# The last eight gate tiles of a hybrid decoder trunk in four Strassen pairs, with half of the convolution's norm beside them and a second order for the head

## The chip, the cores and the metric

The kernel runs on one core of a Trainium2 chip. Times are device microseconds of one execution; the metric is their median over several runs. Differences are given to a tenth of a microsecond. PE is TensorE (matmuls), DVE is VectorE, ACT is ScalarE, POOL is GpSimd, and SP issues the DMAs.

## The reference

One layer of a decoder trunk with three gated branches, over 1024 prompt tokens, 16 meta tokens and 8x8 new tokens (after the meta tokens, 1088 columns that the later stages carry; 1104 with them):

```
u = rmsnorm(h) ;  z = u @ w_in + b_in                 # 1024 -> 6144 columns
a, c, q, k, v, g = split(z)                           # g: 3 x 1024 gate columns
y_a = pool_mixer(a)                                   # windows 2/4/8/16, group maps, scale
y_b = swish(layernorm(depthwise_conv31(glu(c)))) @ w_conv_out
y_c = sliding_window_attention(q, k, v) @ w_attn_out
h = h + (sigmoid(g0)*y_a + sigmoid(g1)*y_b + sigmoid(g2)*y_c) @ w_out
h = h + relu(rmsnorm(h) @ w_up)**2 @ w_down ;  y = rmsnorm(h)
```

All in f32: each factor is split into a high part and a low remainder (both in the fp32r type), and each product is three matmuls, hi x hi, lo x hi and hi x lo.

## The kernel before

Data lie with features on the 128 partitions and tokens along the row. The order of work is written out by hand: Python emits instructions in program order, each engine runs its own in that order, and semaphores hold an instruction until its inputs are there and the buffer that it writes is free. Buffers are `page`s of 1104 f32 out of one pool, given out in program order, so a new page waits for the last reader of the page whose place it takes.

- **Head (0 to 58 us).** `norm1(ci)` is the RMSNorm of token chunk ci (416, 320 and 368 columns) in six steps: steps 0 and 1 square the eight x tiles (L304, ACT) and add them up (L306, DVE); step 2 sums over the partitions with ones-matmuls (L260, tile `st1`), makes rstd columns on DVE, ACT and DVE (L246 to L251) and diagonal tiles of them (L266, `diag`); step 3 broadcasts them by matmuls (L271, `px`); steps 4 and 5 scale x. Between these steps stand the projections: `proj_mm(t, ci)` is the 24 matmuls of input tile t and chunk ci (L151 to L153: 8 k tiles, three matmuls each), `proj_chunk` takes the sum out of PSUM.
- **Input projection (to 706 us).** `w_in` has 48 tiles of 128 columns, each of 3 chunks of 24 matmuls. Tiles 0 to 23 are the branch inputs, 24 to 47 the gates. z tiles go to HBM (`gD`). Beside them lie the attention (`attq`: a queue of slices; `slot(n, d)` runs n slices and then d entries of `dveq`), the new tokens' attention (`sample_slices`, with `SMP` entries of `dveq` after each sequence) and the convolution's 31 taps for each of 4 tiles (`dveq`, L456 and L458: one tap). The last z tiles also split the attention's output for the next stage (`tail_slices`, tiles `oh` and `ol`), and `ln_steps` (the convolution's LayerNorm) runs after them.
- **Output maps, merge and `w_up`.** 8 tiles of `w_ao`, then `w_co`, `w_out`. `w_up` runs as 16 pairs by Strassen's identity in Winograd's form: a 2x2 block product in 7 products instead of 8, each of 24 matmuls of 272 columns (L1470 to L1473), with sums of the operands built on DVE (`sum_pair`, `prep`, L1286 to L1292, L157) and sums of the results taken on DVE (L1612 to L1618).
- **`w_down` (from 1306 us).** 7 products again, of stored operands: `op_load(n, q)` loads operand q of product n, `op_split(n, q)` splits it (`oph` on ACT, `opl` on DVE).

Of the kernel before, what the change touches and what calls it, by code (L numbers as in the profile page):

```python
# [12 lines left out]
P = 128  # L13
# [27 lines left out]
SMP = [0] * 8 + [1] * 6  # L41
# [73 lines left out]
def hybrid_trunk_kernel(ctx, tc, I, O):  # L115
# [46 lines left out]
    jobs = [(I["w_in"][i], 1024, 1 < i < NHEAD) for i in range(48)]  # L162
    WAO = [48, 49] + list(range(51, 57))
    WPOOL = 50
    jobs += [(I["w_ao"][m], 1024, False) for m in range(8)]
# [6 lines left out]
    W = Weights(nc, pool, page, jobs)  # L172
# [270 lines left out]

    def conv_steps(j):
# [17 lines left out]
    def pool_steps(g):  # L462
# [25 lines left out]
        dveq.extend([add(n, 1 << n) for n in range(g + 1)] + [fin])  # L488
# [3 lines left out]
    def ln_steps():  # L492
# [9 lines left out]
        def s2(i):  # L502
            def go():
                a, b = parts[i]
                w, acc = b - a, box["acc"][:, a:b]
                sq = [t[:, o:o + w] for t in [page("lsq") for _ in range(2)] for o in (0, 512)]
                bc = paux()[:, :b - a]
                PE.matmul(bc, lhsT=ones, rhs=acc, start=True, stop=True)
                for j in range(4):
                    V.scalar_tensor_tensor(Y[j][:, a:b], bc, -1.0 / 512, Y[j][:, a:b],  # L510
                                           ALU.mult, ALU.add)
                    A.activation(sq[j], Y[j][:, a:b], AF.Square)
                V.tensor_tensor(acc, sq[0], sq[1], ALU.add)
                V.tensor_tensor(acc, acc, sq[2], ALU.add)
                V.tensor_tensor(acc, acc, sq[3], ALU.add)
# [31 lines left out]
        return [s0, idle, idle, s2(0), s2(1), s2(2),  # L547
                idle, idle, s4(0), s4(1), s4(2), s5(0), s5(1), s5(2)], [s6(j) for j in range(4)]
# [99 lines left out]
    def att_slices(qd):  # L648
# [21 lines left out]
        for n in range(8 * qd, 8 * qd + 8):  # L670
# [3 lines left out]
            out += [(even(n, not first), 1), (odd(n, not first), 1)]  # L674
# [5 lines left out]
    def sample_slices():  # L680
# [3 lines left out]
        def build():  # L684
# [43 lines left out]
        def qk(sq):  # L728
# [7 lines left out]
            lg = page("slg")[:, :192]  # L736
# [119 lines left out]
    def proj_open(ti):  # L856
# [74 lines left out]
    def proj_close(ti):  # L931
# [31 lines left out]
        elif kind == "q":  # L963
# [79 lines left out]
    def tail_slices():  # L1043
        both = lambda *fs: (lambda: [f() for f in fs])
        idle = lambda: None
        pairs = [load_split(Ox, "o", oD[j]) for j in range(8)]
        out = [both(pairs[j][0], pairs[j + 1][0]) for j in (0, 2)]
        for j in range(0, 8, 2):
            fs = [pairs[j][1], pairs[j + 1][1]]
            fs += [pairs[j + 4][0], pairs[j + 5][0]] if j + 4 < 8 else []  # L1050
            out.append((both(*fs), 1))
        return out
# [117 lines left out]
    for m in range(8):  # L1170
# [95 lines left out]


    raws, Ssum, WX = {}, {}, {}
    ORD = ("A11", "S1", "S2", "S4", "S3", "A12", "A22")

    def load_pair(j):
        raws[j] = []
        for f in (2 * j, 2 * j + 1):
            t = page2("wra")[:, :1024] if j % 2 == 0 else \
                pool.tile([P, 1024], F32, name="wraw", tag="wraw", bufs=2)
            SP.dma_start(t, I["w_up"][f])
            raws[j].append(t)

    def sum_pair(j, n):
        a, b = raws[j]  # L1280
        if n == 0:
            Ssum[j] = page2("s12"), page2("s34")
        s12, s34 = Ssum[j]
        S1, S2, S3, S4 = s12[:, :512], s12[:, 512:1024], s34[:, :512], s34[:, 512:1024]
        if n == 0:
            V.tensor_tensor(S1, b[:, :512], b[:, 512:], ALU.add)  # L1286
        elif n == 1:
            V.tensor_tensor(S2, S1, a[:, :512], ALU.subtract)
        elif n == 2:
            V.tensor_tensor(S4, a[:, 512:], S2, ALU.subtract)  # L1290
        else:
            V.tensor_tensor(S3, a[:, :512], b[:, :512], ALU.subtract)  # L1292

    def prep(s):
        j, i = divmod(s, 7)
        a, b = raws[j]
        s12, s34 = Ssum[j]
        src = {"A11": a[:, :512], "A12": a[:, 512:], "A22": b[:, 512:], "S1": s12[:, :512],
               "S2": s12[:, 512:1024], "S3": s34[:, :512], "S4": s34[:, 512:1024]}[ORD[i]]
        tag = ("whi", "wlo")[s % 2]  # L1300
        t = pool.tile([P, 1024], F32R, name=tag, tag=tag, bufs=2)
# [674 lines left out]
```

## Time and profile before

| | |
|---|---|
| median of 3 runs | 1661.78 us (1661.28 to 1661.79) |
| profiled execution | 1662.0 us |
| its span, first to last instruction | 1660.1 us |
| granted TensorE clock, mean | 0.995 |
| busy PE / DVE / ACT | 1642.7 / 1134.5 / 750.5 us |

PE is busy for 99% of the span; the other two engines have room on average, but not everywhere. The profiled execution is 1.9 us longer than its span and 0.2 us longer than the median. Idle time of PE, and matmuls that cost more than their columns, are the two places in which a change shows.

### The profile page before, as it was taken

To read this page: it belongs to the slowest core of one execution; us is meant where nothing else is said; L and a number is where in the kernel's file an instruction comes from. 1 tells how busy PE (TensorE), PEld (TensorE's weight loads), DVE (VectorE), ACT (ScalarE), POOL (GpSimd) and SP (SyncE) were. 2 spreads that over 40 slices of the span, in tenths; PEclk is the share of its full clock that TensorE was granted. 3 is DMA by queue.
4 is the path that set the end of the run, shared out by engine and by line. 5 is a ranking of instruction groups with operands and counts; after the bars stand their busy time and mean duration, and the time that the engine had idled before them with its cause. 6 is when DMAs were issued, how large, how long until landed. Compare 5 with 4: busy or idle time off the path is not lost.

```text
span 1660.1 us, 28943 instructions
## 1 busy us (share of the span) xinstructions
PE 1642.7 (99%) x11568; PEld 1618.2 (97%) x11568; DVE 1134.5 (68%) x2120; ACT 750.5 (45%) x1428; POOL 5.8 (0%) x14
## 2 busy tenths in 40 slices
PE   9999999999999999999999999999999999999997
PEld 8999999999999999999999999999999999999997
DVE  7786767867776666455584687777777844457674
ACT  6537667467675342364243343233332533333341
POOL 0000000000000000000000000000000000000000
PEclk9999999999999999999999999999999999999998
DMA  6051221231225353344253447777776955556652
GB/s 207 15 110 52 71 79 42 68 77 41 81 63 173 97 197 113 104 184 146 80 172 124 152 162 242 244 237 246 243 241 227 323 194 184 183 184 222 204 173 85
DMA packets 132123, 250.78 MB, mean 151 GB/s; under 512 B 33459, under 2 KB 64148, under 8 KB 131988
## 3 DMA queue, kind: packets, MB, share of 16 engines
q1 hardware_dynamic: 131428, 248.45, 46.2%
q8 instruction: 91, 1.49, 0.4%
q10 hardware_dynamic: 560, 0.48, 0.1%
q14 instruction: 44, 0.36, 0.1%
HBM read 168.52 MB, written 80.36 MB: 150 GB/s over the span
## 4 chain that ended last, share of the span: by engine, by line
PE 95%; DVE 2%; ACT 1%; DMA 1%; issue 0%; SPq 0%; DVEq 0%; ACTq 0%
PE pm L151 13%; PE pm L153 13%; PE pm L152 13%; PE m L1663 7%; PE m L1665 7%; PE m L1667 7%; PE m L1470 6%; PE m L1473 6%; PE m L1472 6%; PE pn L151 3%; PE pn L153 3%; PE pn L152 3%; PE px L634 2%; PE px L622 2%; PE qk L581 2%; PE px L271 1%
## 5 line engine op out<-in xcount | busy, mean ns | idle before, releaser
L151 PE MATMUL pm<-uh,whi 128*128 128x320 f32 (+3 forms) x1008 | 338.5, 336 | 0.6 <-ACT uh L342 0.5
L153 PE MATMUL pm<-uh,wlo 128*128 128x320 f32 (+3 forms) x1008 | 333.1, 330 | 0.0
L152 PE MATMUL pm<-ul,whi 128*128 128x320 f32 (+3 forms) x1008 | 332.2, 330 | 0.6 <-DVE ul L343 0.6
L1663 PE MATMUL m<-oph,whi 128*128 128x272 f32 (+2 forms) x896 | 258.5, 289 | 0.0
L1665 PE MATMUL m<-opl,whi 128*128 128x272 f32 (+2 forms) x896 | 258.0, 288 | 0.0
L1667 PE MATMUL m<-oph,wlo 128*128 128x272 f32 (+2 forms) x896 | 257.8, 288 | 0.0
L93 ACT ACTIVATE whi<-wraw 128x1024 fp32r<-128x1024 f32 (+1 forms) x127 | 130.0, 1025 | 205.6 <-PE m L1665 138.3
L94 DVE TENSOR_TENSOR wlo<-wraw,whi 128x1024 fp32r<-128x1024 f32 (+1 forms) x127 | 150.6, 1187 | 98.3 <-ACT whi L93 98.3
L151 PEld LDWEIGHTS pm<-uh,whi 128*128 128x128 f32 x1008 | 190.8, 189 | 2.6 <-ACT uh L342 1.3
L152 PEld LDWEIGHTS pm<-ul,whi 128*128 128x128 f32 x1008 | 191.3, 190 | 1.9 <-DVE ul L343 1.5
L153 PEld LDWEIGHTS pm<-uh,wlo 128*128 128x128 f32 x1008 | 190.3, 189 | 0.4
L1665 PEld LDWEIGHTS m<-opl,whi 128*128 128x128 f32 x896 | 168.8, 188 | 0.0
L1663 PEld LDWEIGHTS m<-oph,whi 128*128 128x128 f32 x896 | 168.6, 188 | 0.0
L1667 PEld LDWEIGHTS m<-oph,wlo 128*128 128x128 f32 x896 | 168.5, 188 | 0.0
L456 DVE SCALAR_TENSOR_TENSOR y<-ext,vec,y 128x1024 f32<-128x1024 f32 x120 | 152.5, 1271 | 0.0
L1470 PE MATMUL m<-bch,wlo 128*128 128x272 f32 x448 | 129.2, 288 | 2.0 <-DVE cb L1614 2.0
L1470 PE MATMUL m<-bch,whi 128*128 128x272 f32 x448 | 129.3, 289 | 0.6 <-DVE h L1409 0.6
L1473 PE MATMUL m<-bch,whi 128*128 128x272 f32 x448 | 128.9, 288 | 0.0
L1473 PE MATMUL m<-bch,wlo 128*128 128x272 f32 x448 | 128.8, 288 | 0.0
L1472 PE MATMUL m<-bcl,whi 128*128 128x272 f32 x448 | 128.7, 287 | 0.0
L1472 PE MATMUL m<-bcl,wlo 128*128 128x272 f32 x448 | 128.7, 287 | 0.0
L1470 PEld LDWEIGHTS m<-bch,wlo 128*128 128x128 f32 x448 | 84.2, 188 | 2.2 <-issue 2.2
(364 smaller groups left out, 3418.1 us busy)
## 6 DMA issues: line engine op xcount, KB each, us to landing
wraw<-w_in SPq DMA_DIRECT2D x46, 512.0 KB, 3.9
opT<-d SPq DMA_DIRECT2D x64, 272.0 KB, 3.0
ld<-opT SPq DMA_DIRECT2D x32, 544.0 KB, 4.6
wd<-w_down SPq DMA_DIRECT2D x32, 512.0 KB, 5.8
sumD<-wd SPq DMA_DIRECT2D x32, 512.0 KB, 4.3
wraw<-sumD SPq DMA_DIRECT2D x32, 512.0 KB, 3.6
gt<-gD SPq DMA_DIRECT2D x24, 544.0 KB, 4.7
ld<-opB SPq DMA_DIRECT2D x23, 544.0 KB, 4.7
```

The costliest lines, as they stand in the source:

```text
L93: self.nc.scalar.activation(hi, r, AF.Copy)
L94: self.late.append(lambda lo=lo, r=r, hi=hi: self.nc.vector.tensor_tensor(lo, r, hi.bitcast(F32), ALU.subtract))
L151: PE.matmul(ps, lhsT=wh[k], rhs=xh, start=first and i == 0, stop=False)
L152: PE.matmul(ps, lhsT=wh[k], rhs=xl, start=False, stop=False)
L153: PE.matmul(ps, lhsT=wl[k], rhs=xh, start=False, stop=last and i == n - 1)
L456: V.scalar_tensor_tensor(y[:, :NP], e[:, k:k + NP], w, y[:, :NP], ALU.mult, ALU.add)
L1470: PE.matmul(ps, lhsT=wh, rhs=xh, start=first and k == 0, stop=False, skip_group_check=True)
L1472: PE.matmul(ps, lhsT=wh, rhs=xl, start=False, stop=False, skip_group_check=True)
L1473: PE.matmul(ps, lhsT=wl, rhs=xh, start=False, stop=k == 3, skip_group_check=True)
L1663: PE.matmul(ps, lhsT=wh[:, w], rhs=xh[:, r], start=k == 0, stop=False, skip_group_check=True)
L1665: PE.matmul(ps, lhsT=wh[:, w], rhs=xl[:, r], start=False, stop=False, skip_group_check=True)
L1667: PE.matmul(ps, lhsT=wl[:, w], rhs=xh[:, r], start=False, stop=k == 15, skip_group_check=True)
```

## The change

1. The z tiles 40 to 47 (gate tiles) become 4 pairs by the same Strassen form as `w_up`: for each pair 7 products of 24 matmuls of 272 columns. Their operands are sums of halves of u over tokens (`z_sums`: 16 DVE operations over four k), split into hi and lo parts (`z_split`; T1 is written over the upper token half of the pages Uh and Ul of k 0 to 3), and sums of weight blocks (`sum_pair`, `prep`). Results go out of PSUM by ACT copies and DVE adds (L1318, L1320, L1322).
2. The attention's odd slots run 2 entries of `dveq` instead of 1; the sample section's `SMP` goes from [0]*8 + [1]*6 to [1]*8 + [2]*6.
3. The loads and splits of the attention's output go from the z tiles into the last pair and the first `w_ao` tile, which for that runs by k over three PSUM banks.
4. `ln_steps` is cut in halves. Its sums and squares (`s0`, six `s2`) run beside the pairs, the rest during `w_ao`.
5. Small tiles move into pages; the attention's pool is closed, and `pool2` opened, before the pairs.
6. In the head, `proj_chunk(3, 0)` and `proj_mm(0, 1)` go ahead of `n1[2]`, `n2[0]`, `n2[1]`, and `proj_mm(2, 1)` ahead of `n1[3]`, `n2[2]`.
7. `op_split(0, 4)` to `(0, 6)` and `op_load(1, 1)` go from the last `w_up` pair into the start of `w_down`.

```diff
-SMP = [0] * 8 + [1] * 6
+SMP = [1] * 8 + [2] * 6
+
+NZP = 4
+NZ = 48 - 2 * NZP
...
-            out += [(even(n, not first), 1), (odd(n, not first), 1)]
+            out += [(even(n, not first), 1), (odd(n, not first), 2)]
...
+    def z_sums(k):
+        ua, ub = zt[k] = page("zu"), page("zu")
+        lo, hi = slice(0, HL), slice(HL, L)
+        for t, n in ((ua, k), (ub, k + 4)):
+            V.tensor_tensor(t[:, :L], Uh[n][:, NM:].bitcast(F32), Ul[n][:, NM:].bitcast(F32),
+                            ALU.add)
+        V.tensor_tensor(ua[:, lo], ua[:, hi], ua[:, lo], ALU.subtract)
+        V.tensor_tensor(ua[:, hi], ub[:, hi], ua[:, hi], ALU.subtract)
+        V.tensor_tensor(ub[:, hi], ub[:, hi], ua[:, lo], ALU.subtract)
+        V.tensor_tensor(ub[:, lo], ub[:, lo], ub[:, hi], ALU.subtract)
...
+        if x == "T1":
+            split(Uh[k][:, NM + HL:], Ul[k][:, NM + HL:], ua[:, lo])
...
+    proj_chunk(3, 0, b0_[3])
+    b1_ = [proj_mm(0, 1)]
     n1[2]()
     n2[0]()
     n2[1]()
-    proj_chunk(3, 0, b0_[3])
-    b1_ = [proj_mm(0, 1)]
     proj_chunk(4, 0, b0_[4])
     b1_.append(proj_mm(1, 1))
+    b1_.append(proj_mm(2, 1))
     n1[3]()
     n2[2]()
-    b1_.append(proj_mm(2, 1))
...
+    load_pair(1 - NZP)
+    for k in range(4):
+        z_split("T1", k)
+    prep(-7 * NZP + 2)
...
+    for s in range(-7 * NZP, 0):
+        j, i = divmod(s, 7)
...
+        if s + 3 < 0:
+            prep(s + 3)
+        if j < -1 and 2 <= i < 6:
+            sum_pair(j + 1, i - 2)
+        b = bk[(0, 1, 0, 1, 0, 2, 0)[i]]
+        product(b, s, i, i in (0, 1, 5), z_comb)
...
+            if i < 3:
+                A.activation(d, ps, AF.Copy)
+            elif i == 6:
+                A.activation(d, ps, AF.Identity, bias=bias_col[1])
+            else:
+                V.scalar_tensor_tensor(d, ps, bias_col[i == 4], d, ALU.add, ALU.add)
...
+            for n in ((), (), (0, 1), (2,), (3,), (4,), (5,))[i]:
+                oq[n][1]()
+            for n in ((0, 1, 2), (), (3, 4), (5,), (6,), (7,), ())[i]:
+                oq[n][0]()
...
+        slot(1, 2)
...
+                if n == q == 0:
+                    op_split(0, 4)
+                    op_load(1, 1)
+                    op_split(0, 5)
+                    op_split(0, 6)
```

**In the head, PE.** Before, the broadcast of chunk 1's rstd (`px_557`, from `diag_482`), the sums over chunk 2's squares (`st1_562`), 24 matmuls of `proj_mm(2, 1)` (`pn_580`), and the broadcast of chunk 2's rstd (`px_611`):

```order
L153 MATMUL pm_532<-uh7_116,wlo_218 128x320
L271 MATMUL px_557<-diag_482,ones_93 128x128 x3
L260 MATMUL st1_562<-ones_93,sq_437 128x1 x3
L151 MATMUL pn_580<-uh0_109,whi_251 128x320
L152 MATMUL pn_580<-ul0_117,whi_251 128x320
...
L153 MATMUL pn_580<-uh7_116,wlo_252 128x320
L271 MATMUL px_611<-diag_576,ones_93 128x128 x3
L151 MATMUL pn_639<-uh0_109,whi_300 128x320
```

After, the same place, where `pn_557` is `proj_mm(2, 1)` and `px_582` is chunk 1's broadcast:

```order
L155 MATMUL pn_557<-ul7_124,whi_251 128x320
L156 MATMUL pn_557<-uh7_116,wlo_252 128x320
L273 MATMUL px_582<-diag_510,ones_93 128x128 x3
L262 MATMUL st1_587<-ones_93,sq_437 128x1 x3
L273 MATMUL px_611<-diag_601,ones_93 128x128 x3
L154 MATMUL pn_639<-uh0_109,whi_300 128x320
```

The 24 matmuls have moved from between `st1` and the second `px` to ahead of the first `px`, so that the three small groups stand next to each other.

**In the head, ACT.** The squares of chunk 2's eight tiles with the engines that each waits for, before:

```order
L304 ACTIVATE sq_437<-x_404 128x368 [waits DMAHW0_49,Activation_49]
L304 ACTIVATE sq_437<-x_404 128x368 x2
L304 ACTIVATE sq_438<-x_406 128x368 [waits DMAHW1_49,Activation_49]
L304 ACTIVATE sq_438<-x_406 128x368 x2
L304 ACTIVATE sq_439<-x_408 128x368 [waits DMAHW2_49,PE_49]
```

and after:

```order
L306 ACTIVATE sq_437<-x_404 128x368 [waits DMAHW0_49,PE_49]
L306 ACTIVATE sq_437<-x_404 128x368 x2
L306 ACTIVATE sq_438<-x_406 128x368 [waits DMAHW1_49,PE_49,Activation_49]
L306 ACTIVATE sq_438<-x_406 128x368 x2
L306 ACTIVATE sq_439<-x_408 128x368 [waits DMAHW2_49,DVE_49]
```

The three pages `sq_437`, `sq_438` and `sq_439` have come to other places in the pool: `sq_438` (squares 4 to 6) and `sq_439` (squares 7 and 8) now take the place of `diag_510`, which PE's `px_582` reads, and `sq_439` also waits for DVE's adds of the squares before it.

**At the entry into the pairs, DVE.** Before, the row between two z tiles holds taps and one weight split. After, this stands there, from the last z tile to the second product; `za` belongs to product 2, `ul` with `zu` is T1, `whi` and `wlo` of 128x512 are the weight operands of products 1 to 4:

```order
L160 TENSOR_TENSOR za_6977<-zu_6802,za_6976 128x544 [waits Activation_49]
L160 TENSOR_TENSOR za_6981<-zu_6867,za_6980 128x544 [waits Activation_49]
L160 TENSOR_TENSOR wlo_6984<-s12_6907,wlo_6984 128x512 [waits PE_49,Activation_49]
L160 TENSOR_TENSOR ul0_117<-zu_6609,uh0_109 128x544 [waits PE_49,Activation_49]
L160 TENSOR_TENSOR ul1_118<-zu_6717,uh1_110 128x544 [waits PE_49,Activation_49]
L160 TENSOR_TENSOR ul2_119<-zu_6801,uh2_111 128x544 [waits PE_49,Activation_49]
L160 TENSOR_TENSOR ul3_120<-zu_6866,uh3_112 128x544 [waits PE_49,Activation_49]
L160 TENSOR_TENSOR whi_7004<-s12_6907,whi_7004 128x512 [waits PE_49,Activation_49]
L1096 TENSOR_TENSOR s34_7007<-wraw_6875,s12_6907 128x512
L1098 TENSOR_TENSOR s34_7007<-wraw_6875,wraw_6877 128x512
L160 TENSOR_TENSOR wlo_7014<-s34_7007,wlo_7014 128x512 [waits PE_49,Activation_49]
```

All of these are new there; each row that waits for "Activation" has an ACT split of the same tile ahead of it, and the T1 rows wait for PE to have read the last z tile's u.

**In pair 2, DVE.** This stands there after (nothing of it before; the norm's steps L526 to L532 then ran during `w_ao`): L526 subtracts the mean, L532 adds squares that ACT made of it, `wlo` and `whi` are weight splits behind ACT, L1094 and L1096 are weight sums, L1322 empties a product's banks:

```order
L526 SCALAR_TENSOR_TENSOR y_3669<-px_7337,y_3669 128x384
L526 SCALAR_TENSOR_TENSOR y_4632<-px_7337,y_4632 128x384
L160 TENSOR_TENSOR wlo_7380<-wra_6994,wlo_7380 128x512 [waits PE_49,Activation_49]
L1094 TENSOR_TENSOR s12_7346<-s12_7346,wraw_7186 128x512 [waits DMAHW1_49,DVE_49]
L1322 SCALAR_TENSOR_TENSOR zc_7264<-zp_7303,b_in_91,zc_7264 128x272 [waits PE_49]
L1322 SCALAR_TENSOR_TENSOR zc_7264<-zp_7304,b_in_91,zc_7264 128x272 [waits PE_49]
L532 TENSOR_TENSOR lacc_7190<-lacc_7190,lsq_7374 128x384 [waits DVE_49] x2
L526 SCALAR_TENSOR_TENSOR y_272<-px_7413,y_272 128x320 [waits PE_49]
L526 SCALAR_TENSOR_TENSOR y_1857<-px_7413,y_1857 128x320
L160 TENSOR_TENSOR whi_7419<-wraw_7186,whi_7419 128x512 [waits Activation_49]
L1096 TENSOR_TENSOR s34_7422<-wraw_7186,s12_7346 128x512
L1322 SCALAR_TENSOR_TENSOR zc_7265<-zp_7266,b_in_91,zc_7265 128x272 [waits PE_49]
```

The evictions of a product have come to stand behind a weight split that waits for ACT, which has two squares to make first.

## Rows read from the trace of the kernel before

**Rows 1.** The page's first parts: the span, busy time and instructions of each engine, and the chain that ended last by engine.

```profile
span 1660.1 us, 28943 instructions
PE 1642.7 (99%) x11568; PEld 1618.2 (97%) x11568; DVE 1134.5 (68%) x2120; ACT 750.5 (45%) x1428; POOL 5.8 (0%) x14
...
PE 95%; DVE 2%; ACT 1%; DMA 1%; issue 0%; SPq 0%; DVEq 0%; ACTq 0%
```

**Rows 2.** PE's waits: tile and line that waited, the engine, tile and line waited for, us in total, times, longest.

```profile
PE m L1470 <- DVE cb L1614: 2.0, 1, 2.0
...
PE st L260 <- DVE sq L306: 1.1, 1, 1.1
PE pn L151 <- DVE gt L1165: 0.8, 1, 0.8
```

**Rows 3.** PE in order of time: the first matmul of a z tile and of the next one; below them the first matmul of a 272-column product of `w_up` and of the next.

```profile
609.99 0.34 PE L151 MATMUL pm<-uh,whi 128*128 128x400 f32 x1
...
621.90 0.34 PE L151 MATMUL pm<-uh,whi 128*128 128x400 f32 x1
...
1021.63 0.28 PE L1470 MATMUL m<-bch,whi 128*128 128x272 f32 x1
...
1024.65 0.29 PE L1470 MATMUL m<-bch,wlo 128*128 128x272 f32 x1
```

**Rows 4.** The head, PE's small groups in order of time.

```profile
34.68 0.80 PE L260 MATMUL st<-ones,sq 128*128 128x1 f32 x6 [1.13 <-DVE sq L306]
44.03 0.83 PE L271 MATMUL px<-diag,ones 128*128 128x128 f32 x6
44.70 0.73 PE L260 MATMUL st<-ones,sq 128*128 128x1 f32 x6
48.90 0.83 PE L271 MATMUL px<-diag,ones 128*128 128x128 f32 x6
```

**Rows 5.** The head, ACT's squares of chunk 2, and DVE's adds of them, evictions and rstd chain, each in order of time.

```profile
37.01 3.30 ACT L304 ACTIVATE sq<-x 128x368 f32<-128x368 f32 x8
...
38.53 4.41 DVE L306 TENSOR_TENSOR sq<-sq 128x368 f32<-128x368 f32 x7
...
45.47 0.16 DVE L246 TENSOR_SCALAR st<-st 128x3 f32<-128x3 f32 x1 [1.54 <-PE st L260]
...
46.70 0.68 DVE L266 TENSOR_SCALAR diag<-ident,st 128x128 f32<-128x128 f32 x3
```

**Rows 6.** Windows: busy us of PE, PEld, DVE, ACT and POOL (with instructions), granted clock, DMA share, GB/s.

```profile
32.00:36.00 4.00, 2.87 (x19) 2.57 (x18) 3.37 (x8) 1.53 (x4) 0.00 (x0) 0.97 0.00 0
36.00:40.00 4.00, 4.00 (x19) 4.00 (x18) 2.92 (x12) 3.88 (x11) 0.00 (x0) 0.60 0.01 2
40.00:44.00 4.00, 4.00 (x29) 4.00 (x28) 3.51 (x7) 0.78 (x2) 0.00 (x0) 1.00 0.00 0
...
1300.00:1304.00 4.00, 1.98 (x16) 1.79 (x16) 4.00 (x6) 1.62 (x2) 0.00 (x0) 1.00 1.03 415
```

**Rows 7.** Attention, DVE in order of time: a tap (L456 and L458) with what follows it.

```profile
147.19 0.43 DVE L587 CUSTOM_DVE_ANT_0 lg<-qk,bias 128x256 f32<-128x256 f32 x1 [1.57 <-PE qk L581]
...
156.95 1.25 DVE L456 SCALAR_TENSOR_TENSOR y<-ext,vec,y 128x1024 f32<-128x1024 f32 x1
158.12 0.28 DVE L458 SCALAR_TENSOR_TENSOR y<-exts,vec,y 128x64 f32<-128x64 f32 x1
158.32 1.22 DVE L94 TENSOR_TENSOR wlo<-wraw,whi 128x1024 fp32r<-128x1024 f32 x1
159.45 0.41 DVE L587 CUSTOM_DVE_ANT_0 lg<-qk,bias 128x256 f32<-128x256 f32 x1
```

**Rows 8.** The sample section in windows, columns as in rows 6.

```profile
500.00:520.00 20.00, 20.00 (x127) 20.00 (x126) 17.95 (x35) 9.50 (x26) 0.00 (x0) 1.00 0.60 186
520.00:540.00 20.00, 20.00 (x134) 20.00 (x133) 10.61 (x51) 10.01 (x31) 0.00 (x0) 1.00 0.57 168
540.00:560.00 20.00, 20.00 (x131) 19.93 (x130) 11.14 (x47) 10.20 (x30) 0.00 (x0) 1.00 0.44 135
560.00:580.00 20.00, 20.00 (x128) 18.73 (x128) 14.76 (x21) 3.78 (x7) 0.00 (x0) 1.00 0.20 65
```

**Rows 9.** Groups of one shape on ACT and DVE, with busy us, mean ns of one and idle time before them: splits of 544 and 512, copies, squares, and the norm's operations.

```profile
L156 ACT ACTIVATE bch<-u 128x544 fp32r<-128x544 f32 x12 | 7.4, 645 | 0.0
L156 ACT ACTIVATE whi<-wraw 128x512 fp32r<-128x512 f32 x8 | 5.0, 623 | 0.0
L928 ACT ACTIVATE zs<-pn,b_in 128x400 f32<-128x400 f32 x4 | 2.4, 596 | 9.6 <-issue 8.8 <-ACT whi L93 0.8
L512 ACT ACTIVATE lsq<-y 128x384 f32<-128x384 f32 x8 | 3.8, 524 | 1.3 <-DVE y L510 1.3
L157 DVE TENSOR_TENSOR wlo<-s,wlo 128x512 fp32r<-128x512 f32 x32 | 22.0, 686 | 0.0
L500 DVE TENSOR_TENSOR lacc<-lacc,y 128x1088 f32<-128x1088 f32 x2 | 2.6, 1294 | 0.1
L510 DVE SCALAR_TENSOR_TENSOR y<-px,y 128x384 f32<-128x384 f32 x8 | 3.9, 550 | 6.7 <-PE px L508 6.7
```

**Rows 10.** The end of `w_up` and the start of `w_down`: PE's first matmul of `w_down`; ACT's loads waited for; DVE in order of time.

```profile
1306.06 0.29 PE L1663 MATMUL m<-oph,whi 128*128 128x272 f32 x1
...
1299.39 1.12 ACT L156 ACTIVATE oph<-ld 128x1088 fp32r<-128x1088 f32 x1 [2.96 <-DMA ld<-opB]
...
1313.34 0.73 DVE L1510 TENSOR_TENSOR d<-cb,d 128x544 f32<-128x544 f32 x1
1313.98 0.72 DVE L1511 TENSOR_TENSOR d<-cb,ca 128x544 f32<-128x544 f32 x1
1314.62 0.72 DVE L1517 TENSOR_TENSOR d<-cb,d 128x544 f32<-128x544 f32 x1
```

More of the change, by code (lines that the diff above doesn't have):

```diff
@@ L160, in hybrid_trunk_kernel @@
     ctx.enter_context(sched)
[L162 to L165, printed above, removed]
+    W = Weights(nc, pool, page, [(I["w_in"][i], 1024, 1 < i < NHEAD) for i in range(NZ)])
+    WAO = [0, 1] + list(range(3, 9))
+    WPOOL = 2
+    jobs = [(I["w_ao"][m], 1024, False) for m in range(8)]
     jobs.insert(WPOOL, (I["w_pool"], 1024, True))
@@ L442, in hybrid_trunk_kernel, with small @@
     sig, ext, Y, ea = {}, {}, {}, {}
+    smalls = {}
+    def small(j, off, n):
+        if j not in smalls:
+            smalls[j] = page("xs")
+        return smalls[j][:, off:off + 8 * n].rearrange("p (s t) -> p s t", s=8)
     def conv_steps(j):
@@ L470, in go @@
                 if n < 2:
-                    box[n] = (page("pt"), apool.tile([P, 8, 23], F32, name="pts", tag="pts", bufs=2))
+                    box[n] = (page("pt"), small(g, 488 + 184 * n, 23))
                 cur, curs = box[(n - 1) % 2] if n else (e, es)
@@ L487, in fin @@
             store(rD[g], r[:, :L])
-        dveq.extend([add(n, 1 << n) for n in range(g + 1)] + [fin])
+        fs = [add(n, 1 << n) for n in range(g + 1)] + [fin]
+        if g == 3:
+            dveq[:0] = fs
+        else:
+            dveq.extend(fs)
     Sx = []
@@ L1041, in load_split, with page2 @@
         return ld, sp
[L1043 to L1052, printed above, removed]
+    def page2(name):
+        return pool2.tile([P, T], F32, name=name, tag="page2", bufs=5)
@@ new lines, in product @@
+    def product(b, s, i, first, op):
+        t = WX.pop(s)
+        for ch in range(2):
+            for k in range(4):
+                wh, wl = (t[:, o + 128 * k:o + 128 * k + 128] for o in (0, 512))
+                xh, xl = op(BX[i], k, ch)
+                ps = b[ch][:, :HL // 2]
+                PE.matmul(ps, lhsT=wh, rhs=xh, start=first and k == 0, stop=False,
+                          skip_group_check=True)
+                PE.matmul(ps, lhsT=wh, rhs=xl, start=False, stop=False, skip_group_check=True)
+                PE.matmul(ps, lhsT=wl, rhs=xh, start=False, stop=k == 3,
+                          skip_group_check=True)
@@ L1146, in hybrid_trunk_kernel @@
             slot(1, NDVE[0] if attq else NDVE[1])
         proj_close(ti)
-    while len(Ox) < 8:
+    while attq:
         slot(1, 1)
+    slot(0)
+    apool_ctx.__exit__(None, None, None)
+    pool2 = ctx.enter_context(tc.tile_pool(name="sb2", bufs=1, reuse_waits="tile"))
+    load_pair(1 - NZP)
+    for k in range(4):
+        z_split("T1", k)
+    prep(-7 * NZP + 2)
+    for n in (2, 3):
+        sum_pair(-NZP, n)
+    for x in ("T3", "T4"):
+        attq.extend(lambda x=x, k=k: [z_split(x, k), z_split(x, k + 1)] for k in (0, 2))
@@ L1265, in comb @@
         return tuple(t[:, o:o + HL // 2] for t in BC[x, k // 2])
[L1268 to L1301, printed above, removed]
-        split(t[:, :512], t[:, 512:], src)
-        WX[s] = t
-        if i == 6:
-            raws.pop(j)
-            Ssum.pop(j)
     sqa = page("sqa")
```

241 lines of the change are left out of this document (178 added, 63 removed).

## The prediction

> **What bounds the kernel now.** I read the page's busy times first: PE works for 1642.7 of 1660.1 us, and PE is 95% of the chain that ended last [rows 1]. So time leaves only through fewer or shorter matmuls, and comes only where PE waits or runs at a lower clock. The view of PE's waits comes next: the longest single one is 2.0 us, and the few above 0.5 us are named there [rows 2]. That is the state in which most of DVE's and ACT's work is hidden, and the question for this change is whether it stays hidden when about 100 DVE and ACT instructions are put beside fewer matmuls. Last I read, stretch by stretch, the head, the attention, the sample section and the two ends of `w_up` in time order.
>
> **The gain.** In the z tiles the first matmul of one tile starts at 609.99 and that of the next at 621.90 [rows 3]: 11.9 us for 72 matmuls. A product of 24 matmuls of 272 columns goes from 1021.63 to 1024.65, 3.0 us [rows 3]. Two tiles are 23.8 us, a pair's seven products 21.1 us. Four pairs: 4 x (23.8 - 21.1) = 10.8; with an even 125 ns for a matmul a pair is 21.0 and the sum 11.3. The starts are rounded to 0.01 us, which is 0.3 over 28 products; I take 11, and 10.5 and 11.7 as bounds. **-11.0.**
>
> The Trainium skill gives another price: "TensorE: Matmul & The Clock Gate", section "Wait — 56ns, not 53.3ns?", has start-to-start of warm matmuls at N / 2.4 GHz + about 2.5 ns. By it a tile would be 11.1 us and a pair 19.5, a gain of 10.6 (an estimate from that page). The trace's 3.02 us for 24 is longer than that rule's 2.78, so here the trace decides, and the sum differs by 0.4.
>
> **The head.** This is in the changed order alone and I am surest of it. Before, PE runs `px` at 44.03, `st` at 44.70, 24 matmuls to 48.90, then the second `px` [rows 4]; nothing waits there.
> - *First stall.* After, `sq_438` and `sq_439` take the place of `diag_510`, so squares 4 to 8 wait for `px_582`. That now stands behind `proj_mm(2, 1)`, directly ahead of `st1_587`, which needs all eight squares added up. What was done in 37.01 to 42.94 beside matmuls [rows 5] now begins when `px_582` ends. Eight squares take 3.30 us, 0.40 each; seven adds take 4.41, 0.63 each [rows 5]. From `px_582`: a square 0.5, adds 4 to 6 in 3 x 0.57 to 0.63, then squares 7 and 8 wait for these adds (0.5), then two adds 1.1 to 1.2: 3.8 to 4.0. **+3.9**, from 0 (were the buffers freed otherwise) to 4.4.
> - *Second stall.* `px_611` follows `st1_587` with no matmuls between. The rstd chain goes from `st`'s end at 45.43 (44.70 + 0.73) to the last `diag` at 46.70 + 0.68 = 47.38 [rows 4, 5]: 1.95 us, covered before by the 24 matmuls, which go up to 48.90. **+2.0**, from 1.5 to 2.6. Those 24 matmuls are not saved: they stand earlier.
> - *Clock.* PE waited 1.13 us before `st` at 34.68; then 36 to 40 us had a granted clock of 0.60 [rows 4, 6]. That stretch did 2.4 us of full-rate work in 4. The 1.13 us wait stays in the changed order, as the matmuls now there wait for the same DVE evictions. A drop after the two new stalls is another (1 - 0.60) x 4 = **+1.6**, from 0 to 3.2: the 2.0 us wait in 1300 to 1304 left a clock of 1.00 [rows 6], so a wait need not bring one.
>
> **Attention.** An odd slot runs a second tap. A tap with its L458 takes 1.4 us by starts (156.95 to 158.32 [rows 7]). Between two visits of the unit's chain to DVE it has room where DVE was idle: 1.57 us ahead of `lg` at 147.19 covers a whole tap [rows 7]. After the tap at 156.95 a weight split and `lg` follow with no gap [rows 7]; there the next `lg`, and the transposes on PE behind it, come 1.4 us later. I count two such places that PE feels: **+2.8**, from 0 to 6. What is put earlier here is taken from a stretch in which PE does not wait, so it gives nothing back.
>
> **Sample section.** 14 more taps, 14 x 1.4 = 19.6 us of DVE, into 500 to 580 us, where DVE is busy for 17.95, 10.61, 11.14 and 14.76 of each 20 [rows 8], 54.5 of 80. In the mean they fit (25.5 free), but DVE is visited several times by each sequence's chain, so a tap delays a visit where it stands ahead of one. Two taps' worth again: **+2.8**, from 0 to 5.
>
> **Entry into the pairs.** T1 overwrites pages that the last z tile reads, so its splits can't start before that tile ends. On ACT then stand the tile's eviction (0.6), two `za` splits (0.57 each), a weight split (0.53) and four T1 splits (0.57 each), these being the durations of [rows 9] less the 0.09 by which neighbours overlap, then DVE's last remainder (0.72): 5.3 us, with the semaphores between some 5.9. Product 0 hides 3.0, and product 1 reads T1's fourth k after 10 matmuls more, 1.25: a wait of about 1.6. Product 2 goes to product 0's banks, whose ACT copies stand behind all that: 0.6 more, and small ones of 0.3. **+2.5**, from 0.5 to 5.
>
> **Pairs 1 to 3.** In pair 1 DVE has 14 splits of 544 (0.64 each, the pitch of [rows 10]), 12 operations of 512 (0.60), four evictions of 272 (0.41, an estimate: 550 ns for 384 and 0.72 us for 544 [rows 9, 10] drawn down to 272) and the norm's three adds of 1088 (1.21): 8.9 + 7.2 + 1.6 + 3.6 = 21.4 us in 21.0 of PE, begun 1.4 late. The three adds stand right ahead of the ones-matmul that sums them, which waits in PE's queue with all products behind it: 1.0. In pair 2 each product has a loop: two mean subtractions (0.47), two squares on ACT behind the first (0.5 each), then ACT's weight split 0.57, DVE's remainder 0.6, a weight sum 0.6, two evictions 0.8, two adds 0.9: about 5 us against 3.0 of PE [rows 3, 9]. Product 6 needs banks that L1322 empties at the end of this loop: 3.0. **+4.0**, from 0 (if the weight splits run ahead) to 8.
>
> **Elsewhere.** `w_ao` has a 0.8 us wait already [rows 2]; the by-k order adds **+0.3**. In `w_down`, `op_split(0, 4)` comes behind the sums of the last pair: 1314.62 + 0.7 [rows 10], less the three splits of 1.2 that no longer stand ahead of them, 1311.7; its own 1.28 gives 1312.9 to 1313.1. PE has 48 matmuls from 1306.06 [rows 10], 6.0 us, and wants it at 1312.1, or a little earlier as the 2.0 wait ahead stays [rows 2]. **+1.0**, from 0 to 2. Costed at nothing: the moved sizes and pages (item 5), which add no instructions, and `z_sums` in the z tiles: 16 operations, 4 x (2 x 1.21 + 4 x 0.64) = 20 us of DVE, over four tiles of 11.9 us, where the taps that are now done earlier (1.4 each) stood; without that cover it would be up to 8.
>
> **The sum.** -11.0 + 3.9 + 2.0 + 1.6 + 2.8 + 2.8 + 2.5 + 4.0 + 0.3 + 1.0 = +9.9. I take +9.5, the stalls being partly the same time (a late DVE in pair 1 is late already from the entry). Span 1669.6, with the 1.9 outside it 1671.5 for a profiled execution; the median is 0.2 lower: **1671 us**.
>
> **The rivals.** A measurement tells 0.2% (3.3 us): faster means under 1658.5, slower over 1665.1.
> - *As forecast* (1666 to 1676): chance 0.50.
> - *The pairs hide their work* (the other side). ACT and DVE have room on average (45% and 68% [rows 1]); if the weight splits run three products ahead of PE, the loop of pair 2 has three products, 9 us, to be late in, and taps lie in idle time. Then only the head and the entry are left: -11.0 + 3.9 + 2.0 + 1.6 + 2.5 = -1.0, 1660.8: not slower. It decides at 3.0 us of loop per product, less whatever lead the splits have. The banks speak against it: they are emptied by rows behind those splits, whatever the lead. Chance 0.13, and 0.03 for a head that is hidden too (1653).
> - *The clock falls again at later stalls.* The windows show one drop after a wait of 1.13 us and none after 2.0 [rows 6]. With stalls at the entry, in pairs 1 and 2 and at `w_down`, four drops at 1.6 add 6.4: 1677.5. Chance 0.22. The Trainium skill, "TensorE: Matmul & The Clock Gate", section "HAM oscillation — how this bites in real kernels", has idle gaps return the gate to half rate; the 0.60 after the head's wait agrees, the 1.00 around 1303 does not.
> - *The late loads.* The last pair's loads of the attention's output compete with four weight loads and stores. ACT waited 2.96 us for such a load at 1299.39 [rows 10]; here its product copies stand behind the split that waits, so one or two such waits reach PE through the banks: +3 to +6, 1675.5. Chance 0.12.
>
> **The numbers.** The range goes from 1662 to 1681: below it stay the two cases in which the work is hidden (0.15), above it only a sum of the second and third rivals. Forecast alone: 1666 to 1676. Faster 0.06, same 0.11, slower 0.83: the case of hidden pairs (1660.8) lies within 0.2%, a quarter of it below, with the hidden head.
>
> **What would show it.** In the profile after: PE waits at `st` L262 for DVE `sq` (about 3.9) and at `px` L273 for `diag` (about 2.0) around 50 us, and a granted clock under 0.7 in the 4 us behind; a wait of L1126 for `ul` or `za` right after the last z tile; waits of the pairs' products for L1322 or L1318; 21.0 us between pairs where they run free. If PE's waits outside the head add up to under 3 us the second rival is right and I am wrong by some 10 us; if the pairs' products take more than 3.0 us where nothing is waited for, the gain is too large in my sum.

## The result, and the profile after

The changed kernel takes 1676.93 us (median of 4, 1675.98 to 1677.95) against 1661.78: slower, ratio 1.0091 with a 95% interval of 1.0073 to 1.0108, so 15 us with 12 to 18. That lies in the range (1662 to 1681), but above the forecast's own 1666 to 1676, and next to the rival in which the clock falls again (1677.5).

The page after (first parts and the chain), which answers to [rows 1]:

```profile
span 1674.2 us, 29251 instructions
PE 1642.2 (98%) x11664; PEld 1612.7 (96%) x11664; DVE 1191.9 (71%) x2220; ACT 767.5 (46%) x1475; POOL 5.7 (0%) x14
...
PE 86%; DVE 7%; ACT 3%; issue 2%; DMA 1%; SPq 0%; DVEq 0%; ACTq 0%
```

PE has 96 matmuls more and as much busy time, and the span is 14.1 us longer: what was added is waiting, and busy time at a lower clock. DVE and ACT have gone from 3% to 10% of the chain that ended last. PE's waits after, which answer to [rows 2]:

```profile
PE st L262 <- DVE sq L308: 4.3, 1, 4.3
PE m L1814 <- DVE opl L160: 3.4, 1, 3.4
PE px L273 <- DVE diag L268: 3.4, 2, 1.7
PE m L1124 <- DVE cb L1765: 2.6, 1, 2.6
PE zp L1124 <- DVE zc L1322: 2.2, 1, 2.2
PE pm L154 <- DVE un L927: 1.6, 1, 1.6
...
PE str L781 <- DVE os L776: 1.0, 1, 1.0
PE px L524 <- DVE lacc L513: 0.9, 1, 0.9
PE zp L1126 <- DVE ul L160: 0.6, 1, 0.6
```

Each wait that the prediction named as a sign is there. When PE comes to the same point of the program in the two traces shows where the time went:

| PE starts | before | after | behind by |
|---|---|---|---|
| the bias matmul after the head | 81.25 | 88.71 | 7.5 |
| the first matmul of the sample section | 516.26 | 526.27 | 10.0 |
| z tile 40, or the first product | 609.99 | 623.25 | 13.3 |
| `w_ao` | 711.07 | 716.25 | 5.2 |
| `w_up` | 963.26 | 971.88 | 8.6 |
| `w_down` | 1306.06 | 1315.53 | 9.5 |
| the end of the span | 1660.1 | 1674.2 | 14.1 |

From `w_ao` to `w_up` the 3.4 us are mostly no loss: the norm's six small groups of matmuls ran among the z tiles before and run here now.

The head after, PE in order of time, which answers to [rows 4]:

```profile
35.01 0.42 PE L154 MATMUL pm<-uh,whi 128*128 128x320 f32 x1 [1.58 <-DVE un L927]
38.66 0.72 PE L262 MATMUL st<-ones,sq 128*128 128x1 f32 x6
46.41 0.83 PE L273 MATMUL px<-diag,ones 128*128 128x128 f32 x6
51.52 1.25 PE L262 MATMUL st<-ones,sq 128*128 128x1 f32 x6 [4.28 <-DVE sq L308]
54.47 1.62 PE L273 MATMUL px<-diag,ones 128*128 128x128 f32 x6 [1.70 <-DVE diag L268]
```

The three groups stand side by side, and before the second and the third of them PE is idle. ACT's squares of chunk 2 in the same stretch:

```profile
47.32 1.31 ACT L306 ACTIVATE sq<-x 128x368 f32<-128x368 f32 x3 [6.30 <-issue]
49.73 0.91 ACT L306 ACTIVATE sq<-x 128x368 f32<-128x368 f32 x2 [1.10 <-DVE sq L308]
```

Squares 4 to 6 begin 0.08 us after the first broadcast ends (46.41 + 0.83), after 6.30 us of idle time, and squares 7 and 8 wait for DVE's adds, in the order that the reused pages ask for (the view names no releaser for the first of the two: "issue"). Windows after, columns as in [rows 6], for the head, the end of the sample section, pair 2 and the start of `w_down`:

```profile
48.00:52.00 4.00, 0.48 (x4) 0.49 (x4) 3.06 (x6) 1.54 (x4) 0.00 (x0) 0.97 0.01 2
52.00:56.00 4.00, 2.30 (x11) 2.24 (x12) 2.30 (x10) 2.01 (x5) 0.00 (x0) 0.50 0.00 0
56.00:60.00 4.00, 4.00 (x21) 4.00 (x21) 3.67 (x8) 2.21 (x5) 0.00 (x0) 0.68 0.06 13
...
576.00:580.00 4.00, 4.00 (x21) 4.00 (x21) 4.00 (x6) 0.00 (x0) 0.00 (x0) 0.67 0.04 12
...
670.00:674.00 4.00, 4.00 (x22) 4.00 (x23) 2.94 (x8) 2.40 (x5) 0.00 (x0) 0.63 0.01 4
...
1322.00:1326.00 4.00, 0.77 (x3) 0.77 (x4) 4.00 (x5) 2.31 (x3) 0.00 (x0) 0.86 0.00 0
1326.00:1330.00 4.00, 4.00 (x26) 4.00 (x25) 4.00 (x5) 1.12 (x1) 0.00 (x0) 0.71 0.86 235
```

The clock is under 1.00 not only behind the head's waits but at three later places; with the neighbouring windows each comes to some 1.7 us of full-rate work not done, 4 x (0.14 + 0.29) for the last one. Two of them begin with the end of a wait, that of 2.2 us in pair 2 and that of 3.4 us in `w_down`. The one at the end of the sample section does not: the wait of 1.0 us is long over there, and what stands directly ahead is a group of 15 small matmuls (`spv`, 574.34 to 576.68).

```profile
565.55 0.33 PE L781 MATMUL str<-ident,os 128*128 128x128 f32 x1 [1.02 <-DVE os L776]
...
574.34 0.49 PE L793 MATMUL spv<-spt,VSh 64*128 64x512 f32 x1
...
577.45 0.51 PE L155 MATMUL pm<-ul,whi 128*128 128x368 f32 x1
```

From 577.4 us on a matmul of 368 columns takes 0.51 us; just before it was 0.33.

### The profile page after: what moved, and what is told of

Same layout as the page of the kernel before. It is cut to its first block, busy times and chain, and to the rows that moved or that the text cites. A ratio compares the mean times of both kernels' runs of the same rounds, so it can differ in the third digit from the quotient of the medians.

```text
span 1674.2 us, 29251 instructions
## 1 busy us (share of the span) xinstructions
PE 1642.2 (98%) x11664; PEld 1612.7 (96%) x11664; DVE 1191.9 (71%) x2220; ACT 767.5 (46%) x1475; POOL 5.7 (0%) x14
## 4 chain that ended last, share of the span: by engine, by line
PE 86%; DVE 7%; ACT 3%; issue 2%; DMA 1%; SPq 0%; DVEq 0%; ACTq 0%
PE pm L154 10%; PE pm L156 10%; PE pm L155 10%; PE m L1814 7%; PE m L1812 7%; PE m L1816 7%; PE m L1124 6%; PE m L1127 6%; PE m L1126 6%; PE pn L154 2%; PE pn L155 2%; PE pn L156 2%; PE px L653 2%; PE px L641 2%; PE qk L600 2%
## 5 line engine op out<-in xcount | busy, mean ns | idle before, releaser
L154 PE MATMUL pm<-uh,whi 128*128 128x320 f32 (+3 forms) x912 | 306.3, 336 | 1.9 <-DVE un L927 1.6
L156 PE MATMUL pm<-uh,wlo 128*128 128x320 f32 (+3 forms) x912 | 301.7, 331 | 0.0
L155 PE MATMUL pm<-ul,whi 128*128 128x320 f32 (+3 forms) x912 | 301.5, 331 | 0.1
L96 ACT ACTIVATE whi<-wraw 128x1024 fp32r<-128x1024 f32 (+1 forms) x119 | 121.7, 1024 | 193.1 <-PE m L1814 142.3
L97 DVE TENSOR_TENSOR wlo<-wraw,whi 128x1024 fp32r<-128x1024 f32 (+1 forms) x119 | 140.8, 1184 | 81.8 <-ACT whi L96 81.8
L154 PEld LDWEIGHTS pm<-uh,whi 128*128 128x128 f32 x912 | 172.8, 189 | 4.1 <-DVE un L927 1.9
L155 PEld LDWEIGHTS pm<-ul,whi 128*128 128x128 f32 x912 | 172.9, 190 | 1.9 <-DVE ul L345 1.6
L156 PEld LDWEIGHTS pm<-uh,wlo 128*128 128x128 f32 x912 | 172.5, 189 | 0.4
```

What stands on the lines that cost most here:

```text
L96: self.nc.scalar.activation(hi, r, AF.Copy)
L97: self.late.append(lambda lo=lo, r=r, hi=hi: self.nc.vector.tensor_tensor(lo, r, hi.bitcast(F32), ALU.subtract))
L154: PE.matmul(ps, lhsT=wh[k], rhs=xh, start=first and i == 0, stop=False)
L155: PE.matmul(ps, lhsT=wh[k], rhs=xl, start=False, stop=False)
L156: PE.matmul(ps, lhsT=wl[k], rhs=xh, start=False, stop=last and i == n - 1)
```

## The experiments

All are held against the kernel before in the same session, by ratio; differences to the changed kernel are of medians.

**The changed kernel once more.** No edit.

> The changed kernel itself, unedited, with more runs beside the kernel before, as the measure that the single edits are held against. From the profile's ledger: PE's waits and the late half-rate stretches cost it 14 us of span against before, so a ratio of 1.0085 to 1.009 (1676 to 1677.5 us). If the half-rate stretches behind its waits at 577, 670 and 1325 us come and go between executions, as the edited kernels let suppose, its runs spread over some 3 to 5 us and the waits stay the same to 0.1 us with other stretches behind them.

Measured: 1677.96 us (1675.88 to 1679.76), ratio 1.0094, 1.0077 to 1.0111. The waits are those above to 0.1 us, but for `opl` with 3.7 and one at the very start (`uh`, 0.9 instead of 0.3), and the clock differs. Two windows of this run:

```profile
576.00:580.00 4.00, 4.00 (x26) 4.00 (x26) 4.00 (x6) 0.00 (x0) 0.00 (x0) 1.00 0.00 0
...
670.00:674.00 4.00, 4.00 (x25) 4.00 (x25) 3.72 (x8) 2.12 (x5) 0.00 (x0) 0.70 0.21 85
```

After the same small matmuls at the end of the sample section the clock stays at 1.00 here and was 0.67 above. The waits belong to the program; where a lower clock follows is in part a matter of the execution.

**The head's order undone.**

```diff
-    proj_chunk(3, 0, b0_[3])
-    b1_ = [proj_mm(0, 1)]
     n1[2]()
     n2[0]()
     n2[1]()
+    proj_chunk(3, 0, b0_[3])
+    b1_ = [proj_mm(0, 1)]
     proj_chunk(4, 0, b0_[4])
     b1_.append(proj_mm(1, 1))
-    b1_.append(proj_mm(2, 1))
     n1[3]()
     n2[2]()
+    b1_.append(proj_mm(2, 1))
```

> The changed kernel with the head in the order of before, all else as changed. Theory of the sum: the head's two stalls (4.3 and 1.7 us in the changed kernel's profile) and one of its two half-rate stretches go, 7.0 to 7.5 us less than the changed kernel, about 1669.5 us; PE's stalls for sq and diag around 50 us are gone. Rival, the pages alone: the moved buffers (item 5) keep the squares behind the broadcast whatever the order; then only the 1.7 us stall goes, about 1674.

Measured: 1667.19 us, ratio 1.0029 (1.0019 to 1.0039), 10 under the changed kernel. The two stalls are gone; of `sq` a wait of 0.21 is left. The order accounts for the loss in the head, and the rival falls. The 2 to 3 us more than expected fit the clock of the profiled execution: this trace has no window under 1.00 in the head (before had one of 0.60), and its wait in pair 2 stands with a full clock behind it. Against that, the wait at the start of `w_down` has grown from 3.4 to 4.4 us.

```profile
658.65 0.36 PE L1124 MATMUL zp<-zb,wlo 128*128 128x272 f32 x1 [2.18 <-DVE zc L1322]
...
660.00:664.00 4.00, 3.82 (x31) 3.61 (x30) 2.91 (x7) 3.06 (x8) 0.00 (x0) 1.00 0.00 0
```

**The head's order alone,** on the kernel before: the same lines the other way round.

> The kernel before with the new order of the head alone. If both stalls come from the order: 7 us over before, about 1669. If the first stall needs the moved pages of item 5 as well, and the second comes from the order: PE waits some 2 us for diag and not for sq, 1.7 to 3.5 us over before (the upper end with a half-rate stretch behind it), 1663.5 to 1665.3.

Measured: 1664.8 us, ratio 1.0019 (1.0010 to 1.0028), about 3 over before. PE waits 1.70 us for `diag` at 51.24 and nowhere for `sq`; the clock stays at 1.00 in 48 to 56. So the second stall is the order's own, and the first needs both the order and the other parts' pages. Which of the small tiles moved into pages decides it was not tried.

**The head's second move undone,** in the changed kernel.

```diff
     b1_.append(proj_mm(1, 1))
-    b1_.append(proj_mm(2, 1))
     n1[3]()
     n2[2]()
+    b1_.append(proj_mm(2, 1))
```

> The changed kernel with proj_mm(2, 1) alone back between the sums of chunk 2 and the second broadcast. Theory of two separate stalls: the 4.3 us wait for sq stays (the squares still need the page that the first broadcast reads), the 1.7 us wait for diag goes: 1.7 less than the changed kernel and up to 1.7 more if the half-rate stretch is shorter, 1673.5 to 1675.2. Rival, one stall: with the matmuls back both go, 6 us less, about 1671.

Measured: 1675.46 us, ratio 1.0070 (1.0055 to 1.0084), 1.5 to 2.5 under the changed kernel. That is just above the expected times, and the six executions spread over 5.5 us (1671.47 to 1676.94), so the waits decide it and not the time. The wait for `sq` is still 4.3, that for `diag` in the head is gone (1.7 of 3.4 is left: that of the final norm, which the kernel before has too). Two separate stalls, as the theory has it.

**The taps alone,** on the kernel before.

```diff
-SMP = [0] * 8 + [1] * 6
+SMP = [1] * 8 + [2] * 6
...
-            out += [(even(n, not first), 1), (odd(n, not first), 1)]
+            out += [(even(n, not first), 1), (odd(n, not first), 2)]
```

> The kernel before with the two numbers that set the taps alone (second tap in the odd slots, the longer list in the sample section). Theory: by PE's milestones the changed kernel lost 2.6 us in the attention and 1.5 in the sample section besides a half-rate stretch; the same shows here, 4.1 over before, to 5.8 with the stretch: 1666 to 1668. Rival, the taps only hurt with the changed pages: within 1.5 us of before.

Measured: 1667.64 us, ratio 1.0027 (1.0018 to 1.0036), 4.5 us over before: the taps' places cost what the table of starting times says (2.5 us in the attention, 3.3 in the sample section, of which 1.7 is the lower clock there), without any of the rest of the change. PE's waits of over 0.1 us between 140 and 600 us in this run:

```profile
PE str L757 <- DVE slg L752: 1.1, 1, 1.1
PE px L622 <- ACT lg L613: 0.3, 1, 0.3
PE px L634 <- DVE pl L157: 0.2, 1, 0.2
```

They add up to less than half of it. The rest lies mostly in the attention, between the small matmuls of the `px` groups: from one to the next of them, 463 times, PE takes 2.0 us more in all than in the kernel before, and few of these gaps are long enough to be listed as waits. The profiled execution, at 1668.11 us, also has a lower clock around 995 us, far from the taps.

**The operand splits back in the last `w_up` pair.**

```diff
-            if i < 4:
+            if i < 5:
                 op_split(0, i)
-            if i < 5:
                 op_load(0, i + 2)
             elif i == 5:
+                op_split(0, 5)
+                op_split(0, 6)
                 op_load(1, 0)
+                op_load(1, 1)
...
-                if n == q == 0:
-                    op_split(0, 4)
-                    op_load(1, 1)
-                    op_split(0, 5)
-                    op_split(0, 6)
```

> The changed kernel with the three operand splits and the load back in the last w_up pair. Theory: the 3.4 us wait at the start of w_down and the 1.7 us that the half-rate stretch behind it costs go, and 0.6 of the wait ahead of it: 5.1 to 5.7 less, about 1671.5. Rival, the late weight tile: the landing that ACT waits 9.4 us for holds the chain either way, and the wait only moves to another operand: within 1.5 us of the changed kernel.

Measured: 1671.64 us, ratio 1.0053 (1.0041 to 1.0066), 5.3 to 6.3 under the changed kernel: the size that the theory gives, and the rival falls. The wait for `opl` is gone. What is left at this place is 2.8 us, on ACT's `oph` in the last pair; the 0.6 us ahead of it did not go, as this wait was 2.6 in the changed kernel. In the profiled execution the lower clock did not go either (0.50 in 1312 to 1316 us, 0.65 in the 4 us behind); it was the slowest of the five, at 1673.89.

**`w_down`'s second weight tile split later.**

```diff
             elif i == 4:
                 W.load_to(3)
-            elif i == 5:
-                W.split_to(2)
-                W.flush()
```

> The changed kernel with the split of w_down's second weight tile after the last pair instead of ahead of its square. Theory of the late tile: in the changed kernel DVE waits 2.7 us for that split (ACT 9.4 us for the landing) ahead of the chain to operand 4; without it there the wait of PE at the start of w_down falls from 3.4 to about 1.0: 2.4 less, 4 with the half-rate stretch gone. Rival, the three operand splits themselves (4.9 us of DVE behind the sums) make the wait: it stays above 3.

Measured: 1673.44 us, ratio 1.0061 (1.0049 to 1.0073), some 4 under the changed kernel; the wait is 2.1, neither 1.0 nor over 3. DVE and ACT around it, in order of time:

```profile
1315.68 1.29 DVE L1627 SCALAR_TENSOR_TENSOR ca<-ca 128x1088 f32<-128x1088 f32 x1
1320.56 0.73 DVE L160 TENSOR_TENSOR opl<-ca,oph 128x544 fp32r<-128x544 f32 x1 [3.59 <-ACT oph L159]
...
1325.08 1.22 DVE L97 TENSOR_TENSOR wlo<-wraw,whi 128x1024 fp32r<-128x1024 f32 x1
...
1319.36 0.62 ACT L1771 ACTIVATE cb<-m 128x544 f32<-128x544 f32 x1 [11.48 <-PE m L1127]
1319.88 0.65 ACT L159 ACTIVATE oph<-ca 128x544 fp32r<-128x544 f32 x1
```

DVE is now early with the square of `ca` and then idle for 3.59 us: the split behind it stands on ACT behind the copy of `cb`, which waits for the last product. From there to the sums and operand 4's split:

```profile
1319.12 0.33 PE L1809 MATMUL m<-oph,whi 128*128 128x272 f32 x1
...
1324.44 0.72 DVE L1667 TENSOR_TENSOR d<-cb,d 128x544 f32<-128x544 f32 x1
...
1326.21 4.89 DVE L160 TENSOR_TENSOR opl<-ld,oph 128x1088 fp32r<-128x1088 f32 x4
```

The last pair's sums end 1325.16 - 1319.12 = 6.0 us after `w_down`'s first matmul; in the changed kernel it is 8.5 (below). So the late tile held them for 2.4 us. The wait falls by 1.3 only, as the edit puts the DVE half of that split (`wlo`, 1.1 us) between the sums and operand 4's split. Without it the wait would be about 0.9 (an estimate, 2.05 - 1.13), near the 1.0 of the first theory; no run shows this.

**The norm beside every second product.**

```diff
-        return [s0, idle, *[s2(*x) for x in six], lambda: box.pop("a")(), idle], [
+        return [s0, idle, idle, *[f for x in six for f in (idle, s2(*x))], idle,
+                lambda: box.pop("a")(), idle], [
```

> The changed kernel with the norm's half steps beside every second product instead of every product, and two products more between the three adds and the sum that needs them. Theory of the loop per product: the waits of 0.9 and 2.2 us and the half-rate stretch behind the second (1.7 us) go, 4.0 to 4.8 less, about 1672.5. Rival, DVE's total work bounds pairs 1 to 3: the waits come back later in the pairs, less than 1.5 us are won.

Measured: 1672.21 us, ratio 1.0061 (1.0048 to 1.0075), about 5 under the changed kernel. Between 610 and 715 us PE has one wait left in the list, that at the entry:

```profile
PE zp L1127 <- DVE ul L160: 0.6, 1, 0.6
```

The work is the same, and its total does not bound the pairs: it was one step in each product. In the changed kernel DVE shows that loop, in pair 2:

```profile
664.07 0.90 DVE L1322 SCALAR_TENSOR_TENSOR zc<-zp,b_in,zc 128x272 f32<-128x272 f32 x2
664.89 1.14 DVE L532 TENSOR_TENSOR lacc<-lacc,lsq 128x384 f32<-128x384 f32 x2
665.95 0.88 DVE L526 SCALAR_TENSOR_TENSOR y<-px,y 128x320 f32<-128x320 f32 x2
667.91 0.69 DVE L160 TENSOR_TENSOR whi<-wraw,whi 128x512 fp32r<-128x512 f32 x1 [1.08 <-ACT whi L159]
668.52 0.68 DVE L1096 TENSOR_TENSOR s<-wraw,s 128x512 f32<-128x512 f32 x1
669.12 0.90 DVE L1322 SCALAR_TENSOR_TENSOR zc<-zp,b_in,zc 128x272 f32<-128x272 f32 x2
```

From one eviction to the next it is 669.12 - 664.07 = 5.05 us, with 1.08 idle for ACT's two squares and split, where PE takes 3.0 for a product. In the kernel before, the same subtractions and squares ran beside the z tiles (the subtractions from 666.4 to 677.1 us), and not during `w_ao` as "The change" has it; no wait of PE is listed there.

**All of it mended.** The edits of the head's order, the operand splits and the norm, and fewer taps:

```diff
-SMP = [1] * 8 + [2] * 6
+SMP = [1] * 6 + [0] * 2 + [1] * 6
...
-            out += [(even(n, not first), 1), (odd(n, not first), 2)]
+            out += [(even(n, not first), 1), (odd(n, not first), 1 if n < 8 else 2)]
```

> The changed kernel with four edits: head in the order of before, operand splits back in the last w_up pair, the norm beside every second product, and fewer taps (a second one in the odd slots only from the second group of heads on; sample list [1]*6 + [0]*2 + [1]*6). Theory, the losses add: 1676.9 less 7 (head), 5 (w_down), 4.5 (norm) and 2.5 (taps), about 1658, 4 us under before. Rival, mended waits move elsewhere (entry, w_ao) or the clock falls behind the ones left: 1662 or more.

Measured: 1653.48 us (1652.16 to 1654.84), ratio 0.9943 (0.9930 to 0.9955): 9 us faster than the kernel before, of the 11.4 that the pairs' matmuls are worth. That is 4.5 us better than the sum in the expectation. The losses add as they were measured singly (10, 5.3 to 6.3 and about 5 us), with the 2.5 us for the fewer taps, which no run measured alone; the changed kernel is 23.4 to 24.5 us slower than this one. PE's waits are near those of [rows 2] again:

```profile
PE m L1125 <- DVE cb L1766: 2.6, 1, 2.6
PE px L273 <- DVE diag L268: 1.7, 1, 1.7
PE st L262 <- DVE sq L308: 1.4, 2, 1.2
...
PE zp L1127 <- DVE ul L160: 0.6, 1, 0.6
```

## Why the prediction was right, and where it was not

| term | forecast | measured in the changed kernel |
|---|---|---|
| the matmuls | -11.0 | -11.4 (pairs 3 and 4 take 42.0 us, 674.29 to 716.25, or 21.0 each) |
| the head, with its clock | +7.5 | +7.5 (4.28 and 1.70 of waits, the rest lower clock and a longer wait for `un`) |
| attention | +2.8 | +2.5 |
| sample section | +2.8 | +1.5, and 1.7 of lower clock |
| entry | +2.5 | +2.2 (the second product takes 5.07 us instead of 3.0) |
| pairs 1 and 2 | +4.0 | +3.1, and 1.7 of lower clock |
| `w_ao` | +0.3 | -0.4 (a wait of 0.4 instead of 0.8) |
| `w_down` | +1.0 | +4.0 (3.4, and 0.6 more ahead of `cb`), and 1.7 of lower clock |
| sum | +9.9 | +14.1 |

- **Right by its steps:** the gain by the trace's own pitches, both stalls in the head with their sizes and causes (the order alone, and the order undone, tell them apart), the wait for T1's remainder at the entry, and the loop of pair 2 ("about 5 us against 3.0"): it is 5.05. For the attention the size came out by luck: the term was two places of one tap each, and the taps alone show no such places, but 2.0 us spread over the matmuls of the `px` groups. For the sample section it was the same assumption, and most of the 1.5 us without the clock is one wait, of 1.0 us ahead of `str`. The taps alone gave 4.5 us for both.
- **Mis-sized: `w_down`.** The step that failed was "less the three splits of 1.2 that no longer stand ahead of them": +1.0 us was forecast, 3.4 of wait came. Before, the last pair's sums ended 1315.34 - 1306.06 = 9.3 us after `w_down`'s first matmul [rows 10]; after, they end 1323.98 - 1315.53 = 8.5 us after it, 0.8 earlier instead of 3.6:

```profile
1315.14 1.06 ACT L96 ACTIVATE whi<-wraw 128x1024 fp32r<-128x1024 f32 x1 [9.38 <-DMA wraw<-w_down]
...
1316.23 1.23 DVE L97 TENSOR_TENSOR wlo<-wraw,whi 128x1024 fp32r<-128x1024 f32 x1 [2.71 <-ACT whi L96]
...
1323.26 0.72 DVE L1667 TENSOR_TENSOR d<-cb,d 128x544 f32<-128x544 f32 x1
1323.90 4.89 DVE L160 TENSOR_TENSOR opl<-ld,oph 128x1088 fp32r<-128x1088 f32 x4
```

What the prediction left out is the split of the second weight tile, which stands ahead of the square of `ca` on DVE and ahead of the copy of `cb` on ACT, and waits for its landing. DVE did come free earlier, and then stood idle for 2.71 us. Before, ACT's half of that split began at much the same place, 0.10 us after `w_down`'s first matmul:

```profile
1306.16 1.06 ACT L93 ACTIVATE whi<-wraw 128x1024 fp32r<-128x1024 f32 x1
```

In the five traces that keep this part of the change (the changed kernel, the same once more, the norm spread, the head's second move undone, the head undone) it begins -0.39, -0.05, +1.00, +1.21 and +1.56 us after that matmul, and in each the sums end 8.84 us later. With the split moved away they end 3.3 us earlier than before, near the 3.6 of the forecast. So the landing held the chain. Why the tile lands when it does was not tried.
- **Taken as a rival, and nearest to the time: the clock.** The forecast counted one stretch, behind the head. There were three more of 1.7 us in the profiled execution, 5.1 together, where the rival had 6.4 for four. That the time comes near the rival's is in part luck: the rival had drops at the entry and in pair 1, where none came, and none in the sample section, where one came. The edited kernels show that it is not a fixed price: the same 2.2 us wait in pair 2 had 0.63 behind it in one kernel and 1.00 in another. The Trainium skill, "TensorE: Matmul & The Clock Gate", section "HAM oscillation — how this bites in real kernels", has long idle gaps bring the half rate. The traces agree in part: in the changed kernel the clock fell at the end of waits of 4.3, 2.2 and 3.4 us (the head, pair 2, `w_down`), but a wait of 2.2 us brought none in one run, at the end of the sample section it fell 11.8 us behind the last listed wait, and in three runs it fell between 994 and 997 us with no wait listed ahead of it, within 1.1 us of the last of 18 matmuls of one column each.
- **The rival on the other side** (the pairs hide their work) fell for the kernel as written, by the loop that it named as its point of decision, and its time shows what it was worth: with the norm beside every second product the loop has 6 us, and of the pairs' waits only that at the entry (0.6 us) is left.
- **The late loads** of the attention's output did not show: no product of the last pair waited, each took 2.98 to 3.01 us.

## What to carry to other kernels

Fewer matmuls are sure time only where the work that makes their operands runs beside them at the pace of one product: count a loop through DVE, ACT and DVE per product and not the engines' totals, and spread added work over every second product when it doesn't fit. A group of small matmuls that depend on each other through another engine wants a block of independent matmuls between each two of them, and moving that block costs the whole chain. When work is taken away ahead of a chain on one engine, ask first what stands next ahead of it: here it was a weight split that waits for its landing, and 0.8 us came of the 3.6 taken away.

## What was not expected of the hardware

A granted clock under 1.00 followed some waits and not others of the same length in the same place: 0.63 and 1.00 behind the wait of 2.2 us in pair 2, in two kernels. It also came without a long wait directly ahead: at the end of the sample section, behind a group of 15 small matmuls, it was 0.67 in one execution of the changed kernel and 1.00 in another, and around 996 us, behind 18 matmuls of one column, it fell in three of the eleven traces. What decides it is not shown here. The times of one kernel spread with it: the changed kernel's first four executions lie within 2.0 us, the four of the second session within 3.9, the five of the mended kernel within 2.7.
